# Strassen's seven block products in w2: two loaded summands move into the hi and lo pools, and the last product changes place

## The chip, the cores and the metric

The kernel runs on one core of a Trainium2 chip. The metric is the time of one execution on the device in microseconds (us), as the median of three runs. Five engines work beside each other: TensorE (PE in the profile) multiplies matrices, VectorE (DVE) and ScalarE (ACT) do element-wise work, GpSimd (POOL) does some copies and issues accumulating loads, and SyncE (SP) issues most of the transfers.

## The reference

The reference is a decoder trunk of two layers over 256 tokens of width 1024, all in float32. A layer is a gated feed-forward block (FFN), a mixer (a gated spatial unit beside differential attention), and a second FFN, each followed by a layer norm with a scaled residual:

```
def _swiglu(x, w1, w3, w2):
    return (jax.nn.silu(x @ w1) * (x @ w3)) @ w2
...
h = _swiglu(x, ffn_w1[l, 0], ffn_w3[l, 0], ffn_w2[l, 0])
x = _layernorm(ALPHA * x + 0.5 * h, ln_g[l, 0], ln_b[l, 0])
```

The hidden width is 2816, that is 22 blocks of 128. This document is about the last product of an FFN, `h @ w2`, with h of 256 x 2816 and w2 of 2816 x 1024. It is computed four times in an execution: in the FFN before and the FFN after the mixer of each of the two layers. They are called FFN 1 to FFN 4 here, in order of time.

## The kernel before

Every float32 weight is multiplied as a sum of two rounded parts. A piece of weights (128 x 1024 values) is loaded into a raw buffer; ACT copies it into a rounded high part, "hi" (L195 and L247 in the profile), and DVE subtracts that from the raw piece and leaves the rest, "lo" (L197 and L249). PE then makes three products: hi with the activations' high part, lo with the high part, hi with the low part. The hi and lo pieces live in two pools, `hi_pool` and `lo_pool`, of eight buffers each (HL = 8); a buffer is free again when the last matmul that reads it is done. The raw buffers are four.

`gemm_seven` (L377 on) computes `h @ w2`. The first eight of the 22 hidden blocks are treated as 2 x 2 blocks and are multiplied by Strassen's algorithm in seven block products (`product`, L369, matmuls on L373) in place of eight; the other 14 blocks are multiplied in the ordinary way (`rows`, L397, matmuls on L402). The output has two halves of 512 columns. In the first half of the stage, block products alternate with `between()`, which multiplies one of the seven ordinary pieces of the first output half (12 matmuls for both groups of 128 tokens, as many as a block product has). They are called P1 to P7 and b1 to b7 here, and the order on PE is

P1 b1 P2 b2 P3 b3 P4 b4 P5 b5 P6 b6 P7 b7, then `done` for the first output half, then the seven ordinary pieces of the second output half (`held`, 84 matmuls).

P1 uses the weights w11 and P2 w21. P3 needs w11+w12 and P4 w11+w12+w22, which DVE adds up in place (`plus`, L356) in the raw buffer r1. For that w12 is loaded as r2 and w22 as r3 (L419 and L426). P5 uses r3 itself, P6 uses r2 after w22 has been added to it by an accumulating transfer that POOL issues (`gather`, L350), and P7 uses r1 after w21 has been added to it in the same manner (L433). So r1, r2 and r3 are loaded tiles that live long.

Before the change r2 and r3 have buffers outside the pools, made in `ffn` under the name `spare`: r2 has two tiles with the tag "val" in the pool `act`, which earlier in the FFN hold results whose halves are transposed; r3 has one tile with the tag "x" in the pool `xs`, which holds half of the FFN's input until the last matmul that reads it. `spare` appears as a tile in the profile. In the first product of an FFN (`seven`, L837) the tiles that correspond to r2 and r3 already live in `hi_pool` and `lo_pool`.

Before a w2 stage stands `gemm_a2` for the two last blocks of w1 and w3: four pieces, whose hi parts are all multiplied first (L295, 32 matmuls) and whose lo parts come after that (L302, 32 matmuls). Before these are the last ordinary pieces of the first product (L283).

The partial sums P1, P3, P4, P6 and P7 are added to the residual in `Norm.fold` (L605, `xtok<-xtok,sbank`, on DVE). P1, P4, P6 and P7 go into the same PSUM bank `bx`, one after the other: what P6 leaves there, `fold` reads, and P7 is then accumulated into the same bank. The matmuls of P7 cannot start before the fold behind P6 has read the bank.

What sets the order of the work: PE runs its instructions in the order in which they are written. On the other engines a planner places the instructions by priorities (`step()` counts them up with each load) and by its own model of when data and buffers are there; a load issues when the planner has a buffer for it, and then waits on the chip until the last reader of that buffer is done. Within the products of an FFN the planner is bound by hand: `line` (L148) chains every hi piece on ACT behind the hi piece before it, and every lo piece and every `plus` on DVE behind the one before it, in the order written. So a `plus` that waits for its load holds up all later lo pieces. The folds, the work on h and the norm are not in this chain; the planner puts them where it expects room. SP issues loads and transposing transfers (L220) from one queue in the planner's order.

`setup` (L539) is a small task of the first FFN alone: it issues loads of constants, then yields, and after 16 beats it computes some constants (L552 to L566). A beat is a count of written matmul work: one block product or one `between()` is one beat.

Of the kernel before, what the change touches and what calls it, by code (L numbers as in the profile page):

```python
# [11 lines left out]
F32 = mybir.dt.float32  # L12
# [8 lines left out]
P = 128  # L21
D = 1024
# [15 lines left out]
HC = CH // 2  # L38
# [16 lines left out]
def trunk(ctx, tc, x, xT, w13a, w13b, w2, wb, wqk, wu, wg, wgr, wbr, wbrr, wo, gateb, gatebr, sgug, sgub, sguwT, sgubias, lam, diffg,  # L55
# [7 lines left out]
    hi_pool = ctx.enter_context(tc.tile_pool(name="hi", bufs=HL))  # L63
    lo_pool = ctx.enter_context(tc.tile_pool(name="lo", bufs=HL))
    xs = ctx.enter_context(tc.tile_pool(name="xs", bufs=2))
# [8 lines left out]
    def name(s):  # L74
        serial[0] += 1
        return f"{s}_{serial[0]}"
# [82 lines left out]
    def fetch(src, width=CH, raw=None):  # L159

        step()
        if raw is None:
            raw = raw_pool.tile([P, CH], F32, tag="raw", name=name("raw"))
        for g in gate:
            g[0] -= 1
        while len(gate) > 1 and gate[1][0] < 0:
            gate.pop(0)
        with behind(gate[0][1] if gate and gate[0][0] < 0 else None):
            if isinstance(raw, list):
                for j, v in enumerate(raw):  # L170
                    loaded[0] = nc.sync.dma_start(v, src[:, j * HC : (j + 1) * HC]).ins
            else:
                loaded[0] = nc.sync.dma_start(raw[:, :width], src).ins
        return raw
# [149 lines left out]
    def gemm_b(src, kts, xh, xl, done, tail=4, last=()):  # L324
# [13 lines left out]
        for t in range(NT):  # L338
            for ps, o, n in blocks[t]:
                for k, piece in held:  # L340
                    rows_b(ps, t, k, piece, xh, xl, kts, o, n)
                done(t, ps[:, :n], o, n)

    def halved(v):
        return v if isinstance(v, list) else [v[:, o : o + HC] for o in range(0, CH, HC)]

# [12 lines left out]
    def pieces(raw):  # L359
        out = []  # L360
        for v in halved(raw):
            hi = hi_pool.tile([P, HC], F32R, tag="hi", name=name("whi"))
            lo = lo_pool.tile([P, HC], F32R, tag="lo", name=name("wlo"))
            for eng, ins in zip((A, V), split(hi, lo, v, after=line[:2])):
                inline(eng, ins)
            out.append((hi, lo))
        return out

    def product(ps, x, w, start, stop):  # L369
        for k in range(4):  # L370
            hi, lo = (v[:, k % 2 * 512 : k % 2 * 512 + 512] for v in w[k // 2])
            for n, (y, o) in enumerate(((hi, 0), (lo, 0), (hi, 1))):
                PE.matmul(ps, x[o](k), y, start=start and k == n == 0, stop=stop and k == 3 and n == 2,  # L373
                          skip_group_check=True)
            beat(0.25)

    def gemm_seven(src, xh, xl, sums, spare, ln, done):  # L377

        q = [[bank(), bank()], [side_bank(), bank()]]
        bx, bz = side_bank(), q[1][0]
        (w11, w21), (w12, w22) = ([s[:, o : o + CH] for o in (0, CH)] for s in src)

        def rest(c):
            for k in range(8, FT, 4):
                nk = min(4, FT - k)
                for j, piece in enumerate(stream(src[c][:, k * 512 : (k + nk) * 512], nk * 512)):
                    yield k + 2 * j, piece

        def rows(t, c, k0, piece, o=0, n=512):  # L397
            for j in range(2):
                k = k0 + j
                hi, lo = (w[:, j * 512 + o : j * 512 + o + n] for w in piece)  # L400
                for m, (y, x) in enumerate(((hi, xh), (lo, xh), (hi, xl))):
                    PE.matmul(q[c][t][:, :n] if o == 0 else more[:, :n], x(k, t), y,  # L402
                              start=k == 8 and m == 0 and (c, t) != (1, 0), stop=k == FT - 1 and m == 2, skip_group_check=True)
            beat(n / 1024)

        def block(t, k0):
            return tuple(lambda k, f=f: f(k0 + k, t) for f in (xh, xl))

        a11, a12, a22 = block(0, 0), block(0, 4), block(1, 4)
        first = rest(0)  # L410

        def between():
            k, piece = next(first)
            for t in range(NT):
                rows(t, 0, k, piece)

        r1 = fetch(w11)
        p1 = pieces(r1)
        r2 = fetch(w12, raw=spare[0])  # L419
        plus(r1, r2)  # L420
        product(bx, a11, p1, True, False)
        ln.fold(0, 0, bx, ALU.add, True)
        between()
        product(q[0][0], a12, pieces(fetch(w21)), False, False)
        gather(r2, w22)
        r3 = fetch(w22, raw=spare[1])  # L426
        between()
        product(bz, sums[0], pieces(r1), True, False)
        ln.fold(1, 1, bz, ALU.add, True)
        between()  # L430
        product(bx, sums[1], pieces(plus(r1, r3)), False, False)
        ln.fold(0, 1, bx, ALU.subtract, True)
        gather(r1, w21)  # L433
        between()
        product(bz, sums[3], pieces(r3), False, False)
        between()
        product(bx, sums[2], pieces(r2), False, False)
        ln.fold(1, 1, bx, ALU.subtract, False)
        between()
        product(bx, a22, pieces(r1), False, True)  # L440
        ln.fold(1, 0, bx, ALU.add, True)
        between()
        for t in range(NT):
            done(t, q[0][t], 0, 512)
        held = list(rest(1))
        line[:] = None, None, False
        cuts = ((0, 512),), (((0, 256), (256, 256)) if ln.last else ((0, 512),))
        for t in range(NT):
            for o, n in cuts[t]:
                more = bank() if o else None  # L450
                for k, piece in held:
                    rows(t, 1, k, piece, o, n)
                done(t, (more if o else q[1][t])[:, :n], 512 + o, n)
# [85 lines left out]
    def setup(after):  # L539
        G.memset(mask[:, :P], 0.0)  # L540
        make_causal_mask(nc, mask[:, P:], NEG)
        lam_t = s512("lam").rearrange("p (l f d) -> p l f d", l=DEPTH, f=4)
        for dst, src in ((x_tok[0], x[:P, :]), (x_tok[1], x[P:, :]), (cos_t, cosT), (sin_t, sinT), (dgs, diffg),
                         (gbh, gateb), (ln_g, lngT), (ln_b, lnbT), (lam_t, lam.partition_broadcast(P))):
            first = dst
            while len(first.shape) > 2:
                first = first[:, 0]
            V.tensor_copy(first[:, :1], after)
            G.dma_start(dst, src)
        yield 16  # L550
        with behind(added[0]):
            V.tensor_scalar(out=gbh, in0=gbh, scalar1=0.5, scalar2=None, op0=ALU.mult)  # L552
        pr = s512("lampr").rearrange("p (l f d) -> p l f d", l=DEPTH, f=4)[:, :, :2]
        for j in range(2):
            with behind(added[0]):
                V.tensor_tensor(out=pr[:, :, j], in0=lam_t[:, :, 2 * j], in1=lam_t[:, :, 2 * j + 1], op=ALU.mult)
        ls = const.tile([P, DEPTH, 2], F32, name="ls")
        V.tensor_reduce(out=ls, in_=pr, op=ALU.add, axis=AX.X)
        A.activation(ls, ls, AF.Exp)
        for l in range(DEPTH):  # L560
            nl = const.tile([P, 1], F32, name=f"neg_lam{l}")
            V.tensor_scalar(out=nl, in0=ls[:, l, 1:2], scalar1=ls[:, l, 0:1], scalar2=-lambda_init(l),
                            op0=ALU.subtract, op1=ALU.add)
            neg_lam.append(nl)
            with behind(added[0]):
                V.tensor_scalar(out=dgs[:, l : l + 1], in0=dgs[:, l : l + 1], scalar1=1.0 - lambda_init(l),  # L566
                                scalar2=None, op0=ALU.mult)
# [175 lines left out]
    def ffn(l, f, i, norm, last=False):  # L743
        xh, xl = parts(both)
# [92 lines left out]
        def seven(src, x_sums):  # L837
# [18 lines left out]
            yield  # L856
            if norm:
                crossed(fetch(w21))
            r2 = fetch(w12, raw=[hi_pool.tile([P, HC], F32, tag="hi", name=name("r2")) for _ in range(2)])
            if norm:  # L860
                yield
            product(bz, x_sums[0], pieces(plus(r1, r2)), True, False)
            A.activation(v1, bz, AF.Copy)
            r3 = fetch(w22, raw=[lo_pool.tile([P, HC], F32, tag="lo", name=name("r3")) for _ in range(2)])
            yield
            product(bx, x_sums[1], pieces(plus(r1, r3)), False, False)
            A.activation(v0, bx, AF.Copy)
# [50 lines left out]
        for j in range(FA, FT - 4, 2):  # L918
            for m, z in gemm_a2([w13a[l, f, j - FA + m] for m in range(2)], both, lambda m: t512("silu")):
# [1 line left out]
                silu[0] = A.activation(s, s, AF.Silu).ins  # L921
                V.tensor_tensor(out=s, in0=s, in1=z[:, T:], op=ALU.mult)
                split(*(v[-1][:, (j - FA + m) * T : (j - FA + m + 1) * T] for v in (h_hi, h_lo)), s)
        spare = [[act.tile([P, D], F32, tag="val", name=name("spare"), bufs=2) for _ in range(2)],
                 xs.tile([P, 4, 512], F32, tag="x", name=name("spare")).rearrange("p k c -> p (k c)")]
        ln = Norm(l, i, 2.0 * ALPHA, 4.0 * EPS, s[:, :1], last)

        def done(t, p, c, n):
# [1 line left out]
            if c + n == D:  # L930
                ln.finish(t, 1.9)

        gemm_seven([w2[l, f, c] for c in range(2)], hh, hl, sums, spare, ln, done)
        return ln.close()

    def mixer(l, i, norm):
# [388 lines left out]
```

## Time and profile before

| | us |
|---|---|
| median of three runs | 1199.31 |
| lowest and highest run | 1195.99, 1201.52 |
| the profiled execution, its own time | 1200.3 |
| its span | 1198.5 |
| PE busy, of the span | 1183.9 |
| DVE busy, of the span | 1012.1 |
| ACT busy, of the span | 824.7 |

The profiled execution lies within the range of the runs, 1.0 us above their median. Some 1.8 us of its time lie outside the span. PE is busy for 99% of the span with a granted clock of 0.999, so time can be found only where PE waits, or in work that PE need not do. A busy time of 512-column matmuls counts overlapping matmuls once; the chain of waits has 12 of them, one block product, in 2.72 us, so in steady work one starts 0.227 us after the other.

The views used below: the waits of an engine (who waited for whom, with total, number and longest); the timeline (start, length, engine, line, and in brackets the idle time just before it and what ended it); the chain of work that ended last (start, length, what); and the table of stretches (busy time of each engine between two times).

### The profile page before, as it was taken

Reading aid. Unit: us, or ns where it says so; the run is one execution under the profiler, and the core shown is the slowest. Engines: PE = TensorE matmul, PEld = TensorE weight load, DVE = VectorE, ACT = ScalarE, POOL = GpSimd, SP = SyncE. Lnnn points to the kernel's source line nnn. Section 1 sums busy time; section 2 is a strip of 40 time slices with the busy share of each in tenths; the row PEclk is TensorE's granted clock in tenths of the full one; section 3 lists DMA queues with packets and bytes.
Section 4 is the critical chain, followed back from the end, with each engine's and each line's share of the span. In section 5 each row is a group of like instructions: output and inputs, shape, how many; then the busy total and the mean of one; then the engine's idle time right before and its main releaser. Section 6 shows DMA issues by size and latency. Waiting matters only on the chain.

```text
span 1198.5 us, 16639 instructions
## 1 busy us (share of the span) xinstructions
PE 1183.9 (99%) x5771; PEld 993.0 (83%) x5771; DVE 1012.1 (84%) x1558; ACT 824.7 (69%) x1418; POOL 299.4 (25%) x356
## 2 busy tenths in 40 slices
PE   9999999999999999999999999999999999999998
PEld 7888778888888888887788888888888888888877
DVE  6889989888688989879899879888965989989795
ACT  6688658559955677885677886576788556679860
POOL 1112301137430220071020071003564112102500
PEclk9999999999999999999999999999999999999999
DMA  9969885757855758698668698676666754886870
GB/s 350 284 193 283 257 285 192 265 198 212 248 205 186 226 180 272 198 284 241 240 205 270 173 290 253 230 270 239 210 204 211 252 182 165 259 252 212 269 236 36
DMA packets 129220, 276.14 MB, mean 230 GB/s; under 512 B 89024, under 2 KB 90096, under 8 KB 104560
## 3 DMA queue, kind: packets, MB, share of 16 engines
q1 hardware_dynamic: 121392, 248.80, 62.3%
q0 software_dynamic: 7312, 25.76, 9.1%
q8 instruction: 45, 0.74, 0.2%
q10 hardware_dynamic: 432, 0.52, 0.1%
q14 instruction: 39, 0.32, 0.1%
HBM read 249.10 MB, written 1.05 MB: 209 GB/s over the span
## 4 chain that ended last, share of the span: by engine, by line
PE 84%; DMA 6%; DVE 5%; ACT 3%; issue 1%; POOL 0%; SPq 0%; ACTq 0%; DVEq 0%; POOLq 0%
PE bank L283 43%; PE bank L295 13%; PE sbank L373 8%; PE bank L302 7%; PE bank L402 6%; PE sbank L402 3%; DMA raw<-in_w 3%; DVE wlo L197 2%; PE bank L512 2%; PE sbank L984 1%; DMA spare<-in_w 1%; DVE wlo L249 1%; DMA planes<-planes 1%; ACT whi L195 1%; ACT whi L247 1%
## 5 line engine op out<-in xcount | busy, mean ns | idle before, releaser
L197 DVE TENSOR_TENSOR wlo<-raw,whi 128x1024 fp32r<-128x1024 f32 (+1 forms) x374 | 414.5, 1136 | 52.5 <-ACT whi L195 38.1
L195 ACT ACTIVATE whi<-raw 128x1024 fp32r<-128x1024 f32 (+1 forms) x378 | 351.8, 959 | 135.1 <-PE bank L283 43.7
L283 PE MATMUL bank<-whi,x 128*128 128x512 f32 x1224 | 386.3, 390 | 0.0
L283 PEld LDWEIGHTS bank<-whi,x 128*128 128x128 f32 x1224 | 229.8, 188 | 47.8
L283 PE MATMUL bank<-wlo,x 128*128 128x512 f32 x612 | 238.2, 389 | 0.0
L295 PE MATMUL bank<-x,whi 128*128 128x512 f32 x640 | 153.3, 391 | 0.0
L295 PEld LDWEIGHTS bank<-x,whi 128*128 128x128 f32 x640 | 118.2, 188 | 23.8
L283 PEld LDWEIGHTS bank<-wlo,x 128*128 128x128 f32 x612 | 114.9, 188 | 23.2
L247 ACT ACTIVATE whi<-raw 128x1024 fp32r<-128x1024 f32 (+1 forms) x96 | 92.4, 983 | 60.2 <-DVE raw L356 35.1
L249 DVE TENSOR_TENSOR wlo<-raw,whi 128x1024 fp32r<-128x1024 f32 (+1 forms) x96 | 110.1, 1161 | 12.5 <-ACT whi L247 12.3
L229 POOL COPY seven<-seven 128x512 uint16<-128x512 uint16 x16 | 67.1, 4253 | 105.9 <-ACT whi L195 54.5
L302 PEld LDWEIGHTS bank<-x,wlo 128*128 128x128 f32 x640 | 81.4, 191 | 2.9
L302 PE MATMUL bank<-x,wlo 128*128 128x256 f32 x640 | 82.6, 283 | 0.0
L402 PE MATMUL bank<-whi,hhi 128*128 128x512 f32 (+1 forms) x182 | 68.3, 375 | 0.8 <-DVE silu L305 0.8
L402 PE MATMUL bank<-whi,hlo 128*128 128x512 f32 (+1 forms) x182 | 67.9, 373 | 0.0
L402 PE MATMUL bank<-wlo,hhi 128*128 128x512 f32 (+1 forms) x182 | 67.9, 373 | 0.0
L960 POOL TENSOR_TENSOR swap<-swap,sin_t 128x512 f32<-128x512 f32 x16 | 25.9, 1618 | 103.4 <-DMA swap<-z 59.3
L719 POOL COPY nvia<-ntwo 128x256 uint16<-128x256 uint16 x20 | 9.9, 539 | 159.1 <-DMA ntwo<-nvia 108.0
L303 ACT ACTIVATE r<-bank 128x256 f32<-128x256 f32 x96 | 34.0, 372 | 12.9 <-PE bank L302 12.8
L373 PE MATMUL sbank<-whi,xhs 128*128 128x512 f32 x128 | 42.0, 389 | 0.0
L402 PEld LDWEIGHTS bank<-whi,hhi 128*128 128x128 f32 x182 | 34.3, 188 | 7.2 <-DVE silu L305 1.3
L402 PEld LDWEIGHTS bank<-whi,hlo 128*128 128x128 f32 x182 | 34.3, 188 | 6.1
(286 smaller groups left out, 2159.1 us busy)
## 6 DMA issues: line engine op xcount, KB each, us to landing
raw<-in_w13b SPq DMA_DIRECT2D x68, 1024.0 KB, 5.5
raw<-in_w SPq DMA_DIRECT2D x32, 1024.0 KB, 6.4
raw<-in_wb SPq DMA_DIRECT2D x16, 1024.0 KB, 5.5
raw<-in_wqk SPq DMA_DIRECT2D x16, 1024.0 KB, 5.7
r<-in_w13b SPq DMA_DIRECT2D x16, 512.0 KB, 5.9
raw<-in_w13a SPq DMA_DIRECT2D x8, 1024.0 KB, 4.8
raw<-in_wgr SPq DMA_DIRECT2D x8, 1024.0 KB, 5.4
raw<-in_wg SPq DMA_DIRECT2D x8, 1024.0 KB, 5.1
```

What stands on the lines that cost most here:

```text
L195: inline(A, A.activation(h, r, AF.Copy).ins)
L197: low = eng.tensor_tensor(out=w, in0=r, in1=h.bitcast(F32), op=ALU.subtract).ins
L229: eng.tensor_copy(out=o, in_=i)
L247: a = A.activation(hi, src, AF.Copy).ins
L249: return a, eng.tensor_tensor(out=lo, in0=src, in1=hi.bitcast(F32), op=ALU.subtract).ins
L283: PE.matmul(ps, xx, w, start=start and n == 0, stop=stop and n == 2)
L295: PE.matmul(b[-1], hi[:, k * P : (k + 1) * P], xc(k), start=k == 0, stop=False)
L302: PE.matmul(b[n][:, :T], lo[:, k * P : (k + 1) * P], xc(k)[:, :T], start=False, stop=k == KT - 1)
L303: emptied[0] = A.activation(r[:, s], b[n][:, T:], AF.Copy, scale=scale).ins
L373: PE.matmul(ps, x[o](k), y, start=start and k == n == 0, stop=stop and k == 3 and n == 2, skip_group_check=True)
L402: PE.matmul(q[c][t][:, :n] if o == 0 else more[:, :n], x(k, t), y, start=k == 8 and m == 0 and (c, t) != (1, 0), stop=k == FT - 1 and m == ...
L960: turned_by[0] = G.tensor_tensor(out=s3, in0=s3, in1=s, op=ALU.mult).ins
```

## The change

It has three parts. First, the tiles of r2 (two of 128 x 1024) are taken from `hi_pool` and those of r3 (two of 128 x 1024) from `lo_pool`, by a new function `homes`; `spare` and its three tiles go. r3 is then loaded by two transfers of 512 KB in place of one of 1 MB. `seven` calls the same function for the tiles that it already had there, which changes nothing in it. Second, `between()` with b7 stands ahead of P7, so that the order on PE becomes ... P6 b6 b7 P7, `done`, `held`. Third, `setup` yields for 22 beats in place of 16.

```diff
+    def homes(pool, tag):
+        return [pool.tile([P, HC], F32, tag=tag, name=name("home")) for _ in range(2)]
...
-    def gemm_seven(src, xh, xl, sums, spare, ln, done):
+    def gemm_seven(src, xh, xl, sums, ln, done):
...
         p1 = pieces(r1)
-        r2 = fetch(w12, raw=spare[0])
+        r2 = fetch(w12, raw=homes(hi_pool, "hi"))
         plus(r1, r2)
...
         gather(r2, w22)
-        r3 = fetch(w22, raw=spare[1])
+        r3 = fetch(w22, raw=homes(lo_pool, "lo"))
         between()
...
         product(bx, sums[2], pieces(r2), False, False)
         ln.fold(1, 1, bx, ALU.subtract, False)
         between()
+        between()
         product(bx, a22, pieces(r1), False, True)
         ln.fold(1, 0, bx, ALU.add, True)
-        between()
         for t in range(NT):
             done(t, q[0][t], 0, 512)
...
-        yield 16
+        yield 22
         with behind(added[0]):
             V.tensor_scalar(out=gbh, in0=gbh, scalar1=0.5, scalar2=None, op0=ALU.mult)
...
-        spare = [[act.tile([P, D], F32, tag="val", name=name("spare"), bufs=2) for _ in range(2)],
-                 xs.tile([P, 4, 512], F32, tag="x", name=name("spare")).rearrange("p k c -> p (k c)")]
...
-        gemm_seven([w2[l, f, c] for c in range(2)], hh, hl, sums, spare, ln, done)
+        gemm_seven([w2[l, f, c] for c in range(2)], hh, hl, sums, ln, done)
```

More of the change, by code (lines that the diff above doesn't have):

```diff
@@ L858, in seven @@
                 crossed(fetch(w21))
-            r2 = fetch(w12, raw=[hi_pool.tile([P, HC], F32, tag="hi", name=name("r2")) for _ in range(2)])
+            r2 = fetch(w12, raw=homes(hi_pool, "hi"))
             if norm:
@@ L863, in seven @@
             A.activation(v1, bz, AF.Copy)
-            r3 = fetch(w22, raw=[lo_pool.tile([P, HC], F32, tag="lo", name=name("r3")) for _ in range(2)])
+            r3 = fetch(w22, raw=homes(lo_pool, "lo"))
             yield
```

## The prediction

> **What bounds the kernel now.** I read the busy times first, then who PE waited for, then a table of the four w2 stages, and then the chain and the timeline in them. The page's row of busy times says that PE is busy nearly all the time:
>
> ```profile
> PE 1183.9 (99%) x5771; PEld 993.0 (83%) x5771; DVE 1012.1 (84%) x1558; ACT 824.7 (69%) x1418; POOL 299.4 (25%) x356
> ```
>
> The change removes no matmul, so it can only win back PE's waits. Whom PE waited for (total, number, longest):
>
> ```profile
> PE sbank L373 <- DVE xtok L605: 3.4, 3, 1.4
> ...
> PE sbank L373 <- ACT whi L247: 1.3, 1, 1.3
> PE sbank L373 <- DVE wlo L249: 1.2, 2, 0.8
> ...
> PE bank L402 <- DVE silu L305: 0.8, 1, 0.8
> ```
>
> All four rows lie in `product` and `rows`, that is in w2 stages (L373 is shared with the FFN's first product). How much each stage loses comes from four stretches, each from the first matmul of P1 to the first matmul behind the stage (FFN 1 to FFN 4; length, then PE, PEld, DVE, ACT, POOL):
>
> ```profile
> 124.50:186.69 62.19, 58.76 (x258) 47.47 (x257) 54.59 (x84) 38.45 (x58) 7.67 (x9) 1.00 0.75 254
> 540.57:602.39 61.82, 59.03 (x259) 47.55 (x258) 55.52 (x78) 36.23 (x54) 5.08 (x7) 1.00 0.72 234
> 719.60:777.51 57.91, 57.91 (x259) 47.79 (x258) 52.94 (x76) 34.85 (x52) 3.01 (x6) 1.00 0.76 250
> 1131.12:1190.34 59.22, 58.42 (x297) 49.27 (x296) 47.70 (x68) 25.88 (x35) 3.40 (x6) 1.00 0.51 160
> ```
>
> FFN 3 has no idle PE at all: 57.91 us is the stage's floor at the same granted clock of 1.00. Against it FFN 1 loses 4.28, FFN 2 3.91 and FFN 4 1.31 us (its last tile is cut in two, so a little of that is not a wait). Together 9.5 us: that is the ceiling of any gain here, 0.8% of the kernel.
>
> **Part one: b7 ahead of P7.** The chain of waits shows what holds P7 up in FFN 2 (start, length, what):
>
> ```profile
> 560.93 8.54 DMA raw<-in_w
> ...
> 569.55 1.07 ACT whi L247
> ...
> 571.79 1.74 DVE wlo L197 x2
> ...
> 574.06 2.35 DVE wlo L197 x2
> 576.42 0.61 DVE xtok L605
> ...
> 577.16 2.97 PE sbank L373 x12
> 580.13 2.72 PE bank L402 x12
> ```
>
> The accumulating load into r1 lands 8.54 us after its issue; P7's pieces, which are ahead of b7's in the chained order, wait for it, the following pieces pile up behind, and the fold behind P6 runs only after four of them. P7 needs the bank that this fold reads. Its own pieces, done before the 571.79 us row, had been ready for five microseconds. The same wait in FFN 1 and FFN 4, as the timeline gives it:
>
> ```profile
> 161.63 0.47 PE L373 MATMUL sbank<-whi,hhi 128*128 128x512 f32 x1 [1.34 <-DVE xtok L605]
> ...
> 577.16 0.47 PE L373 MATMUL sbank<-whi,hhi 128*128 128x512 f32 x1 [1.41 <-DVE xtok L605]
> ...
> 1165.22 0.47 PE L373 MATMUL sbank<-whi,hhi 128*128 128x512 f32 x1 [0.61 <-DVE xtok L605]
> ```
>
> Idle 3.36 us in all. With b7 in between, P7 is due 2.72 us later (the 12 matmuls of b7 in the chain above), so a fold that keeps its place is done 1.3 us ahead of need in FFN 2 (2.72 less the wait of 1.41). Term one: -3.4 us. Bounds: -3.4, and 0 if the planner moves the fold back by as much.
>
> What moves with it: b7's load, its hi and lo now precede P7's two pieces in the chain, which takes DVE's idle time in front of the late load away, and b7 no longer waits for it. The cover is ample: in the chain above b7's lo starts at 571.79, and b7 is now due at 575.6 (576.96 less the wait of 1.41 us). r1's raw buffer is given up some 2 us later, so one load for the second output half goes out that much later on SP; its piece is due only after several others of 12 matmuls each. On POOL nothing is passed. `fold`, then both `part`s, come in one burst on DVE behind P7, five operations with their statistics at 0.61 us (the fold's row) or little more, while PE runs 84 matmuls on other banks: hidden; without that cover some 3 us. I take 0.
>
> **Part two: r2 and r3 in the pools.** In FFN 2 the second tile of r2 becomes free late, and DVE stands still until its load has come:
>
> ```profile
> 531.55 1.23 DVE L356 TENSOR_TENSOR raw<-raw,spare 128x1024 f32<-128x1024 f32 x1 [0.57 <-DMA spare<-in_w]
> ...
> 534.36 0.57 SPq L171 DMA_DIRECT2D spare<-in_w  x1
> ...
> 540.44 1.23 DVE L356 TENSOR_TENSOR raw<-raw,spare 128x1024 f32<-128x1024 f32 x1 [7.07 <-DMA spare<-in_w]
> ...
> 717.10 1.23 DVE L356 TENSOR_TENSOR raw<-raw,spare 128x1024 f32<-128x1024 f32 x1 [5.26 <-DMA spare<-in_w]
> ```
>
> The last row is FFN 3. There the load comes 2.50 us ahead of P1's start (717.10 against 719.60), in FFN 2 0.13 us ahead (540.44 against 540.57): 2.37 us later, and FFN 2's loss beside the fold is 3.91 - 1.41 = 2.50 us. So DVE's lateness goes into PE's time one for one.
>
> With the change r2 needs two of eight hi buffers. Ahead of it in written order stand four pieces of `gemm_a2` and two of P1; the other two are those of the matmuls on L283, which end where L295 begins. From the chain (FFN 3):
>
> ```profile
> 708.68 7.25 PE bank L295 x32
> 715.93 3.83 PE bank L302 x32
> ```
>
> So the second load of r2 can leave SP by 708.7 in FFN 3, and by the same distance, 10.9 us ahead of P1 (719.60 - 708.68), at 529.6 in FFN 2 in place of 534.36: 4.7 us sooner. That is more than the 2.37 us which FFN 2 lacks. I take -2.0 there, -0.5 in FFN 4 (1.31 less 0.61, not all a wait), 0 in FFN 3. Bounds: -2.5 and -0.7; on the other side a later r2, priced as a rival below.
>
> r3 now needs two lo buffers, free when the pieces of L302 are read, in place of the input's tile, which is free after all of L302. Its two loads are each half as long:
>
> ```profile
> spare<-in_w SPq DMA_DIRECT2D x8, 512.0 KB, 5.9
> ...
> spare<-in_w SPq DMA_DIRECT2D x4, 1024.0 KB, 9.4
> ```
>
> They land some 3.5 us sooner (9.4 - 5.9). PE waits for r3 nowhere, so 0; one issue more on SP is some 0.57 us (the issue's row above) of SP's queue, in which no load stands that PE waits for here.
>
> The cost: six hi buffers for the pieces while r2 lives, and six lo buffers while r3 does. P4's second piece then takes the hi buffer that b2 gives up. b2 ends one product and one `between()` ahead, so the buffer is free 5.4 us (2 x 2.72) before P4 starts; ACT's 1.07 and some 1.2 of DVE (1.74 and 2.35 us for two, in the chain) make 2.3 us. Every later piece has at least as much. So 0, with 2.3 us for each pair of pieces as the price if that cover goes.
>
> The trace has one more price. A lo piece takes 1.21 us, but in FFN 1 the one that starts at 119.5, while POOL copies until 120.2, takes 1.73:
>
> ```profile
> L197 DVE TENSOR_TENSOR wlo<-raw,whi x2: 1212/1470/1727, 119.5 to 121.2; 128x1024 fp32r<-128x1024 f32 x2
> ...
> 117.67 2.57 POOL L229 COPY seven<-seven 128x512 uint16<-128x512 uint16 x2 [3.37 <-DMA seven<-seven]
> ...
> 712.57 2.85 POOL L229 COPY planes<-planes 128x512 uint16<-128x512 uint16 x4
> ```
>
> In FFN 3 POOL's four copies (the last row) fall into the 5.26 us in which DVE stands still, in FFN 2 and 4 likewise; the sooner load puts DVE's work there. Four operations longer by 0.52 us make 2.1 us of DVE, inside the time gained. I take 0.5 us for PE in FFN 2 to 4 together (0 to 2.1 each).
>
> [...]
>
> **Part three: `setup` six beats later.** Today its operations stand in DVE's queue ahead of P4's sum, in FFN 1, and P4 waits for that:
>
> ```profile
> 129.53 0.41 DVE L552 TENSOR_SCALAR gbh<-gbh 128x32 f32<-128x32 f32 x1
> 129.80 0.20 DVE L566 TENSOR_SCALAR dgs<-dgs 128x1 f32<-128x1 f32 x2
> ...
> 133.03 0.48 DVE L556 TENSOR_TENSOR lampr<-lam 128x128 f32<-128x128 f32 x2
> ...
> 133.77 0.41 DVE L558 TENSOR_REDUCE ls<-lampr 128x4 f32<-128x256 f32 x1
> ...
> 137.75 0.33 DVE L562 TENSOR_SCALAR neg_lam<-ls 128x1 f32<-128x1 f32 x2
> ...
> 142.26 0.50 PE L373 MATMUL sbank<-whi,sum 128*128 128x512 f32 x1 [1.25 <-ACT whi L247]
> 143.53 0.50 PE L373 MATMUL sbank<-wlo,sum 128*128 128x512 f32 x1 [0.76 <-DVE wlo L249]
> ```
>
> 0.41 + 0.20 + 0.48 + 0.41 + 0.33 = 1.83 us of DVE. Six beats are three block products and three `between()`s, 16 us, so they come at about 146 us, behind P4's pieces. FFN 1's loss beside the fold is 4.28 - 1.34 = 2.94 us. Against this, r2 comes later here: its second load leaves by 111.14 us today, and with hi buffers by 113.6, 10.9 us ahead of P1's 124.50. The rows are the issue (with its length to the end of the second), the two sums, and DVE's idle time before P4:
>
> ```profile
> 107.34 3.80 SPq L171 DMA_DIRECT2D spare<-in_w  x2
> ...
> 116.74 2.88 DVE L356 TENSOR_TENSOR raw<-raw,spare 128x1024 f32<-128x1024 f32 x2
> ...
> 132.69 0.42 DVE L249 TENSOR_TENSOR hlo<-silu,hhi 128x256 fp32r<-128x256 f32 x1 [1.22 <-ACT hhi L247]
> ```
>
> The delay of 2.5 us meets 1.22 us in which DVE stands still, so 1.3 us remain. I take -1.8 + 1.3 = -0.5 us, and -0.9 more for the short gaps within P4 (2.94 less 1.25 and 0.76), which a P4 with pieces at hand does not have: -1.4. Bounds -2.9 and +1.3.
>
> **Sum.** -3.4 - 2.0 - 0.5 + 0.5 - 1.4 = -6.8 us. I allow +0.6 for restarts of a planner's order that I cannot see, one wait like the smallest above (0.61): -6.2. The profiled execution took 1200.3, so 1194.1 on its own time; it lies 1.0 above the median of 1199.31, so the median to expect is 1193.1.
>
> **The rivals.** (A) *r2 comes later, not sooner.* The planner may hand r2 the last hi buffers, those that L295 reads, and not those of L283. Its second load then leaves when L295 ends: in FFN 2 at 536.9, 3.7 us ahead of P1 (719.60 - 715.93), against 534.36 today: 2.5 us later. In FFN 3 it leaves at 715.93; today, with the 6.1 us that the load takes in FFN 2 (534.36 to 540.44), at 711.0: 4.9 later, and the same in FFN 4. In FFN 1 at 120.8 against 111.14: 9.7. Together 22.0 us, passed on one for one, less 3.4 and 1.8: 1200.3 + 16.8 = 1217. For it: a load competes with conversions that the planner would rather have early. Against: r2's load has no data to wait for, and the FFN's first product keeps such tiles in these pools with no wait of PE in the table above. It ends slower by 0.5% if r2 is later by 3 us on average over the four stages (12 us, less 5.2 of gains, is over 6.0). (B) *Only the fold's wait is won.* DVE is busy 55.52 of 61.82 us in FFN 2; if it stays the limit, P4's waits come back at b3 or P5: 1200.3 - 3.4 = 1196.9, a median of 1196. Against: FFN 3 has DVE work of 52.94 and no wait. (C) *The move does nothing.* The fold is not chained, and the planner may put it as far back as P7 went: only parts two and three remain, -3.4 + 0.6, so 1197.5 and a median of 1196.5.
>
> **How the numbers follow.** Forecast 0.60, A 0.15, B 0.16, C 0.09. A measurement of this kernel tells about 0.5%, 6.0 us, from no change. The forecast's own width is 1189.8 (the ceiling of 9.5 us) to 1196, and 0.37 of its 0.60 lie below 1193.3; its other 0.23, B, C and 0.03 of A, where r2 is late by a little, are within 0.5%; 0.12 of A is slower. That makes 0.37, 0.51, 0.12. The range runs from the ceiling, 1189.8, to 1202, which takes in B and C and the mild end of A and leaves out some 0.15.
>
> **What would show it.** P7's first matmul without a wait for L605; DVE's waits for r2's load, 7.07 and 5.26 us in FFN 2 and 3, below 2; r2's second load leaving SP no later than L295's start; P4 in FFN 1 waiting under 1.5 us; the four stretches at 58 to 60 us. The forecast is wrong if a stretch other than FFN 1 exceeds 60 us, if ACT's or DVE's pieces wait for matmuls of L295 or b2 while PE waits for them, or if FFN 3, which has nothing to win, becomes longer by over 1 us.

## The result and the profile after

| | before | after |
|---|---|---|
| median, us (20 runs each) | 1201.52 | 1195.28 |
| lowest and highest run | 1195.99, 1207.13 | 1193.83, 1197.62 |
| ratio of after to before | | 0.995, interval 0.9936 to 0.9963 |
| the profiled execution, its own time | 1200.3 | 1197.46 |
| its span | 1198.5 | 1195.7 |

The change won 6.2 us, 0.5%, and the runs lie closer together: 3.8 us apart instead of 11.1. The before kernel's median was 1199.31 over its first three runs and is 1201.52 over twenty. The profiled execution of after is one of its slowest, 2.2 us above its median: its losses are not those of every execution.

On the page of after the row of busy times shows as many matmuls as before, and PE busy for 1.4 us longer:

```profile
PE 1185.3 (99%) x5771; PEld 994.5 (83%) x5771; DVE 1012.0 (85%) x1558; ACT 826.2 (69%) x1418; POOL 286.1 (24%) x356
```

Of the waits of PE these two are all that is left in the w2 stages (total, number, longest). No row names the fold any more (it was L605 and is L608 now):

```profile
PE bank L376 <- DVE wlo L249: 3.9, 3, 1.9
...
PE sbank L376 <- DVE wlo L249: 0.6, 1, 0.6
```

The table of the same four stretches, each from P1 to the end of the stage (length, then PE, PEld, DVE, ACT, POOL, the granted clock, the share of DMA, GB/s):

```profile
124.14:185.50 61.36, 58.78 (x259) 47.38 (x257) 56.35 (x87) 38.48 (x56) 4.76 (x7) 1.00 0.77 245
539.51:597.22 57.71, 57.71 (x258) 47.63 (x257) 52.98 (x76) 36.20 (x53) 4.47 (x7) 1.00 0.79 251
714.55:772.50 57.95, 57.95 (x259) 47.63 (x258) 53.21 (x77) 35.86 (x51) 3.28 (x5) 1.00 0.78 251
1126.27:1188.14 61.87, 59.91 (x297) 50.47 (x296) 50.21 (x70) 28.18 (x35) 4.20 (x6) 0.97 0.52 158
```

FFN 2 fell from 61.82 to 57.71 and now has no idle PE. FFN 3 stayed. FFN 1 fell by only 0.83, and FFN 4 *rose*, from 59.22 to 61.87. Together the stages won 2.3 of the span's 2.8 us. Where a stage is said to lose so much below, it is the sum over its matmuls of what each starts later than at the steady spacing (0.227 us for 512 columns, 0.12 for 256); by that, to about 0.1 us, FFN 1 to 4 lost 4.6, 3.9, 0.1 and 1.5 us before and 3.7, 0.1, 0.3 and 4.1 after.

What FFN 4 lost is a new wait at P2, and something behind it. The timeline of PE (start, length, what, and the idle time before with what ended it) and the table of 4 us stretches around it:

```profile
1133.46 0.40 PE L376 MATMUL bank<-whi,hhi 128*128 128x512 f32 x1
1135.74 0.50 PE L376 MATMUL bank<-wlo,hhi 128*128 128x512 f32 x1 [1.89 <-DVE wlo L249]
...
1137.11 0.63 PE L376 MATMUL bank<-whi,hlo 128*128 128x512 f32 x1
1137.54 0.63 PE L405 MATMUL bank<-whi,hhi 128*128 128x512 f32 x1
```

```profile
1132.00:1136.00 4.00, 2.04 (x8) 1.31 (x8) 3.88 (x9) 3.99 (x8) 0.00 (x0) 1.00 0.97 350
1136.00:1140.00 4.00, 4.00 (x12) 3.09 (x12) 4.00 (x6) 1.80 (x2) 1.10 (x2) 0.57 1.03 395
```

P2's second piece has no lo part yet, and PE stands still for 1.89 us. Then the matmuls start 0.43 us apart instead of 0.23: the granted clock over the second stretch of 4 us is 0.57. Some eight matmuls, each 0.2 us late, make the extra 1.6 us, and they count as busy time.

Why the lo part is late is seen on SP's queue, here in FFN 2 and in FFN 4:

```profile
527.26 0.33 SPq L171 DMA_DIRECT2D home<-in_w  x1
528.37 4.00 SPq L220 DMA_TRANSPOSE planes<-planes  x2
532.49 0.50 SPq L171 DMA_DIRECT2D home<-in_w  x1
```

```profile
1114.02 0.33 SPq L171 DMA_DIRECT2D home<-in_w  x1
1115.64 4.71 SPq L220 DMA_TRANSPOSE planes<-planes  x2
1120.45 0.53 SPq L171 DMA_DIRECT2D home<-in_w  x1
```

and on VectorE at the sum that waits for the second load:

```profile
536.17 2.19 DVE L359 TENSOR_TENSOR raw<-raw,home 128x1024 f32<-128x1024 f32 x1 [2.38 <-DMA home<-in_w]
```

```profile
1125.76 1.23 DVE L359 TENSOR_TENSOR raw<-raw,home 128x1024 f32<-128x1024 f32 x1 [3.90 <-DMA home<-in_w]
```

The second load of r2 stands behind two transposing transfers on SP, and goes out 0.1 us after the second of these has been issued. In FFN 2 that is 7.02 us ahead of P1, in FFN 4 5.82. The sum then starts 3.34 us ahead of P1 in FFN 2 and 0.51 us ahead in FFN 4 (1126.27 - 1125.76). Every lo piece behind it in the chained order is late with it. In FFN 1 P2 waits in the same way (idle 0.95 and 1.01 us); there the second load went out 6.5 us ahead of P1:

```profile
117.59 0.53 SPq L171 DMA_DIRECT2D home<-in_w  x1
...
130.95 0.50 PE L376 MATMUL bank<-wlo,hhi 128*128 128x512 f32 x1 [0.95 <-DVE wlo L249]
...
133.62 0.49 PE L376 MATMUL bank<-wlo,hhi 128*128 128x512 f32 x1 [1.01 <-DVE wlo L249]
```

### The profile page after: what moved, and what is told of

Read it like the earlier page. It is cut to its first block, busy times and chain, and to the rows that moved or that the text cites. A ratio compares the mean times of both kernels' runs of the same rounds, so it can differ in the third digit from the quotient of the medians.

```text
span 1195.7 us, 16657 instructions
## 1 busy us (share of the span) xinstructions
PE 1185.3 (99%) x5771; PEld 994.5 (83%) x5771; DVE 1012.0 (85%) x1558; ACT 826.2 (69%) x1418; POOL 286.1 (24%) x356
## 4 chain that ended last, share of the span: by engine, by line
PE 92%; DVE 4%; DMA 2%; issue 1%; ACT 1%; SPq 0%; DVEq 0%; ACTq 0%
PE bank L283 44%; PE bank L295 14%; PE sbank L376 10%; PE bank L405 9%; PE bank L302 7%; PE sbank L405 3%; PE bank L515 1%; DVE wlo L197 1%; PE sbank L985 1%; DMA home<-in_w 1%; DVE wlo L249 1%; DMA raw<-in_w13b 1%; PE bank L376 1%; PE sbank L1041 1%; PE sbank L1159 1%
## 5 line engine op out<-in xcount | busy, mean ns | idle before, releaser
L197 DVE TENSOR_TENSOR wlo<-raw,whi 128x1024 fp32r<-128x1024 f32 (+1 forms) x374 | 414.7, 1134 | 52.8 <-ACT whi L195 38.0
L283 PE MATMUL bank<-whi,x 128*128 128x512 f32 x1224 | 386.5, 390 | 0.0
L283 PEld LDWEIGHTS bank<-whi,x 128*128 128x128 f32 x1224 | 229.8, 188 | 47.7
L283 PE MATMUL bank<-wlo,x 128*128 128x512 f32 x612 | 238.3, 389 | 0.0
L295 PE MATMUL bank<-x,whi 128*128 128x512 f32 x640 | 153.3, 391 | 0.0
L295 PEld LDWEIGHTS bank<-x,whi 128*128 128x128 f32 x640 | 118.2, 188 | 23.8
L283 PEld LDWEIGHTS bank<-wlo,x 128*128 128x128 f32 x612 | 114.9, 188 | 23.4
L229 POOL COPY seven<-seven 128x512 uint16<-128x512 uint16 x16 | 55.9, 3554 | 115.6 <-ACT whi L195 60.8
L359 DVE TENSOR_TENSOR raw<-raw,home 128x1024 f32<-128x1024 f32 x32 | 40.4, 1273 | 25.1 <-DMA home<-in_w 22.0
```

The costliest lines, as they stand in the source:

```text
L197: low = eng.tensor_tensor(out=w, in0=r, in1=h.bitcast(F32), op=ALU.subtract).ins
L229: eng.tensor_copy(out=o, in_=i)
L283: PE.matmul(ps, xx, w, start=start and n == 0, stop=stop and n == 2)
L295: PE.matmul(b[-1], hi[:, k * P : (k + 1) * P], xc(k), start=k == 0, stop=False)
L359: inline(V, V.tensor_tensor(out=v, in0=v, in1=m, op=ALU.add).ins)
```

## The experiments

Each kernel was run in five rounds. Ratios are to the before kernel on the same chip, with their 95% interval.

**Each part alone.** First the move of b7, on the before kernel:

```diff
+        between()
         product(bx, a22, pieces(r1), False, True)
         ln.fold(1, 0, bx, ALU.add, True)
-        between()
```

> The kernel before with b7 ahead of P7 and nothing else changed. Theory (the parts add up): P7's waits for the fold (idle 1.34, 1.41 and 0.61 us in FFN 1, 2 and 4 before) are gone and all other waits stay: 3.4 to 3.8 us less, ratio 0.997. Rival (the planner moves the fold back by one piece as well): P7 still waits for L605 by more than 1 us in two stages, no change.

Measured: 1197.53 us, 0.9964 (0.994 to 0.9987), that is -4.3 us, with runs from 1191.75 to 1202.32. No stage has a wait at P7. The profiled execution, 1200.51 us, is above its median: in FFN 3 r2's load came late (its sum waited for it until 717.13, P1 had begun at 715.83), and b1 waited. The bank that b1 writes is read first by L305, which stands on VectorE behind that sum and two lo pieces:

```profile
721.02 0.50 PE L402 MATMUL bank<-whi,hhi 128*128 128x512 f32 x1 [2.28 <-DVE silu L305]
```

Then `setup` alone on the before kernel:

```diff
-        yield 16
+        yield 22
```

> The kernel before with setup's pause of 22 beats in place of 16 and nothing else changed. Theory (its 1.8 us of VectorE stand ahead of P4's sum): P4 in FFN 1 waits 2.0 us less or so and the other stages are as before: 1 to 2 us less, ratio 0.999. Rival (VectorE is late at P4 for other reasons): P4's two waits of 1.25 and 0.76 us stay, no change.

Measured: 1201.41 us, 1.0006 (0.9984 to 1.0027). No change that can be told. In FFN 1 what P4 lost did fall, from 2.7 to 1.0 us, but r2's load was late in FFN 3 and FFN 4 of this execution, and b1 waited there for 1.1 and 2.7 us.

Then the homes of r2 and r3 alone (`homes` and its calls from the change's diff, with b7 and the 16 beats as before):

```diff
-        r2 = fetch(w12, raw=spare[0])
+        r2 = fetch(w12, raw=homes(hi_pool, "hi"))
...
-        r3 = fetch(w22, raw=spare[1])
+        r3 = fetch(w22, raw=homes(lo_pool, "lo"))
```

> The kernel before with r2 and r3 in the pools and nothing else changed. As predicted (r2 never later than today but in FFN 1, by 2.5 us): 2 to 3 us less, FFN 2's stretch shorter by 2 us and more, FFN 4 not longer. Theory from the trace after (the planner puts r2's second load behind the transposing transfers on SP's queue, so r2 comes 5 to 6 us later against P1 in FFN 1 and 2 us later in FFN 4): P2 waits 2 us or so in FFN 1 and again in FFN 4, FFN 2 gains 2 to 2.5 us, so 0 to 3 us more, ratio 1.000 to 1.002.

Measured: 1199.92 us, 0.9987 (0.9969 to 1.0006), runs from 1197.29 to 1201.47. In the waits of PE the fold is still there, and the waits at P2 have come:

```profile
PE bank L376 <- DVE wlo L249: 3.3, 2, 2.3
PE sbank L376 <- DVE xtok L608: 2.7, 3, 1.3
```

So the three parts alone are worth -4.3, +0.7 and -1.6 us by their ratios (0.9964, 1.0006 and 0.9987 of 1201.5). They add up to -5.2, within the interval of the whole change (-7.7 to -4.4). The move is the one part whose gain alone can be told from nothing.

**One part undone.** The move undone in the after kernel (b7 behind P7 again):

> The changed kernel with b7 back behind P7. Theory: P7 waits for the fold again in two to four stages, 3 to 4.5 us more than the changed kernel's 1195.3, 1198.5 to 1200. Rival (with r2 earlier VectorE is ahead anyway and the fold is in time): 1195.3.

Measured: 1198.83 us, 0.9979 (0.9963 to 0.9994), 3.5 us above the after kernel. The fold's waits are back:

```profile
PE sbank L376 <- DVE xtok L608: 1.9, 2, 1.3
```

`setup` undone (`yield 22` to `yield 16` in the after kernel):

> The changed kernel with setup's pause of 16 beats as before. Theory (its 1.8 us of VectorE come back ahead of P2 to P4 in FFN 1, as the kernel with the pools alone has them): FFN 1 loses 5 to 6 us in place of 3.7, and with a wait of more than 2 us the halved clock for 3.4 us, 1196.5 to 1198. Rival (no part of it matters): 1195.3.

Measured: 1195.58 us, 0.9957 (0.994 to 0.9974). My number of 1196.5 and more was wrong: the six beats bring nothing that can be told here. The timeline of VectorE in FFN 1 of the after kernel suggests why:

```profile
138.74 0.17 DVE L555 TENSOR_SCALAR gbh<-gbh 128x32 f32<-128x32 f32 x1
...
139.69 1.22 DVE L359 TENSOR_TENSOR raw<-raw,home 128x1024 f32<-128x1024 f32 x1
...
141.42 0.33 DVE L565 TENSOR_SCALAR neg_lam<-ls 128x1 f32<-128x1 f32 x2
141.66 1.22 DVE L359 TENSOR_TENSOR raw<-raw,home 128x1024 f32<-128x1024 f32 x1
```

The planner did not put `setup` behind P4's sums (139.69 and 141.66) but right ahead of the first and between the two. It still stands in P4's way; it only stands there closer.

r2 back in the two "val" tiles, the rest as in the after kernel:

```diff
-        r2 = fetch(w12, raw=homes(hi_pool, "hi"))
+        r2 = fetch(w12, raw=spare)
...
+        spare = [act.tile([P, D], F32, tag="val", name=name("spare"), bufs=2) for _ in range(2)]
```

> The changed kernel with r2 back in the two tiles of the pool act, r3 still in lo_pool. Theory (what the pools bring is r2's steadier and mostly earlier landing): r2's second sum falls anywhere from 2.6 us before P1's start to 2 us after it, b1 or P4 wait again by 1 to 3 us in one or two stages, median 1197 to 1198 and single runs more than 6 us apart. Rival (r3's earlier load is what counts): as the changed kernel, 1195.3.

Measured: 1200.1 us, 0.9996 (0.9974 to 1.0018), with runs from 1195.13 to 1207.5. So r2's home is worth 4.8 us beside the other parts, more than I gave it. The profiled execution shows where it goes: FFN 1 is better than in the after kernel (0.8 us lost against 3.7), FFN 4 has

```profile
1128.31 1.23 DVE L359 TENSOR_TENSOR raw<-raw,spare 128x1024 f32<-128x1024 f32 x1 [8.36 <-DMA spare<-in_w]
```

with P1 at 1127.11, and PE waits at b1 for 2.2 us; the granted clock over 1126 to 1188 us is 0.97, in the other stages 1.00. This kernel has the move too, and yet is no faster than before, where the move alone won 4.3 us. The two intervals overlap between 0.9974 and 0.9987; whether r3's home or `setup` costs something while r2 is in the "val" tiles was not run. One thing that differs from a good stage is how long the transposing transfers ahead of the load take. The table of DMA issues in a short stretch has the median time from issue to landing in its last column; here it is for FFN 4 of this kernel:

```profile
spare<-in_w SPq DMA_DIRECT2D x1, 512.0 KB, 7.4
planes<-planes SPq DMA_TRANSPOSE x2, 6.1
```

for FFN 2 of the before kernel, where VectorE stood still for 7.07 us:

```profile
spare<-in_w SPq DMA_DIRECT2D x1, 512.0 KB, 6.0
planes<-planes SPq DMA_TRANSPOSE x2, 6.3
```

and for its FFN 3, where the sum was in time:

```profile
spare<-in_w SPq DMA_DIRECT2D x2, 512.0 KB, 5.5
...
planes<-planes SPq DMA_TRANSPOSE x2, 3.4
```

The transposing transfers take 3.4 us or 6.3 in one and the same execution, and r2's load goes out behind them. The load itself takes longer too: the second of the two in FFN 3 landed in 5.1 us (the 5.5 is the median of both), that of FFN 2 in 6.0. Over all kernels the spread of the runs goes with r2's home: with r2 in the "val" tiles it is 11.1, 10.6, 10.0 and 12.4 us (before, the move alone, `setup` alone, this one), with r2 in the hi pool 1.1 to 6.3 us (all the others), over 6 to 20 runs each. That r2's late load is behind the spread in the runs without a profile is an inference.

r3 back in the tile of `xs` (one load of 1 MB), the rest as in the after kernel:

```diff
-        r3 = fetch(w22, raw=homes(lo_pool, "lo"))
+        r3 = fetch(w22, raw=spare)
```

> The changed kernel with r3 back in the tile of the pool xs, loaded in one piece of 1 MB, r2 in hi_pool. Theory (PE waits for r3 nowhere): as the changed kernel, 1195.3 within 1 us. Rival (with r2 earlier, VectorE reaches P4's sum before r3 has landed): P4 waits by 1 us or more in FFN 2 or 3, over 1196.5.

Measured: 1197.49 us, 0.9963 (0.9949 to 0.9977); the intervals of this and of the after kernel overlap. I had expected no difference beyond 1 us, and it came out 2.2 us slower. The profiled execution's waits are at P2 and P4 in FFN 1 and in FFN 4. The loss is thus not only where r3 is used, and its cause stays open.

**r2's load ahead of the transposing transfers.** If the queue on SP is what makes r2 late, then a load that is written ahead of P1's pieces, and so is planned before the transposing transfers, should take P2's waits away:

```diff
         r1 = fetch(w11)
-        p1 = pieces(r1)
         r2 = fetch(w12, raw=homes(hi_pool, "hi"))
+        p1 = pieces(r1)
```

> The changed kernel with r2 fetched ahead of P1's conversions, so that r2 takes the earlier hi buffers and both its loads stand ahead of the transposing transfers on SP's queue. Theory (r2's late landing is what P2 waits for in FFN 1 and FFN 4): the sum of w11+w12 starts 4 to 6 us earlier against P1, the waits at P2 are gone, 3 to 5 us less than the changed kernel's 1195.3, ratio 0.991 to 0.993 to the kernel before. Rival (VectorE's own work ahead of P2 is the cause): P2 waits as before, 1195. Second rival (P1's pieces, now behind r2, come late): P1 waits instead, over 1195.

Measured: 1193.59 us, 0.9943 (0.992 to 0.9966), with runs only 1.1 us apart. Both loads now leave together, 16.3 us ahead of P1 in all four stages; in FFN 2:

```profile
523.48 1.30 SPq L171 DMA_DIRECT2D home<-in_w  x2
...
529.07 1.23 SPq L220 DMA_TRANSPOSE planes<-planes  x1
```

P2 waits in no stage, and FFN 2 to 4 lose no more than 0.1 us each. FFN 1 lost 4.7, in a new way: b1 waits for L305 to have read its bank, and on VectorE L305 stands behind a lo piece that ran while GpSimd copied (the second row is a summary of line L197: shortest, median and longest, in ns):

```profile
130.10 0.50 PE L405 MATMUL bank<-whi,hhi 128*128 128x512 f32 x1 [2.71 <-DVE silu L305]
```

```profile
L197 DVE TENSOR_TENSOR wlo<-raw,whi x2: 1214/2696/4179, 123.3 to 124.4; 128x1024 fp32r<-128x1024 f32 x2
```

```profile
124.44 3.10 POOL L229 COPY planes<-planes 128x512 uint16<-128x512 uint16 x4
```

The subtraction that starts at 124.4 takes 4.18 us instead of 1.21, and ends 1.0 us behind the last of the four copies.

**The copies moved from GpSimd to ACT**, on top of the last kernel (L792 of the after kernel: who joins the halves of the last front):

```diff
-  yield from transposed(s, p, s, lead, wait - lead, 2.6, A if n < 3 else G, to, A if n else G)
+  yield from transposed(s, p, s, lead, wait - lead, 2.6, A if n != 3 else G, to, A if n else G)
```

> The kernel that fetches r2 first, with the last front's four copies after its transposing transfers on ScalarE in place of GpSimd. Theory (a VectorE subtraction waits out GpSimd's copies: 4.18 us in place of 1.21 ahead of b1 in FFN 1): b1's wait of 2.9 us in FFN 1 and the halved clock behind it are gone, no VectorE subtraction above 2 us there, 3 to 4.5 us less than the 1193.6 of that kernel, 1189 to 1190.5. Rival (VectorE is late at b1 for its own work, or ScalarE now is): FFN 1 keeps a wait of 2 us or more, 1193 and over.

Measured: 1192.46 us, 0.9931 (0.9914 to 0.9948). The wait at b1 is gone, and the two subtractions take what they take elsewhere:

```profile
122.69 2.35 DVE L197 TENSOR_TENSOR wlo<-raw,whi 128x1024 fp32r<-128x1024 f32 x2
```

The four stretches of this execution, in the same columns as above, are all but at the floor except for FFN 1, where P4 still waits for 1.3 us:

```profile
124.62:183.85 59.23, 58.29 (x259) 47.54 (x257) 54.14 (x85) 40.83 (x62) 4.24 (x6) 1.00 0.82 267
538.06:595.71 57.65, 57.65 (x259) 47.70 (x257) 50.60 (x74) 37.10 (x55) 4.26 (x6) 1.00 0.76 250
713.07:770.71 57.64, 57.64 (x258) 47.70 (x257) 50.57 (x73) 36.56 (x53) 2.83 (x4) 1.00 0.76 252
1124.49:1182.41 57.92, 57.92 (x296) 49.41 (x295) 46.11 (x66) 29.18 (x39) 3.37 (x5) 1.00 0.53 165
```

The median gained only 1.1 us on the kernel before it, less than I had expected. The same edit on the after kernel itself, with r2's load where it was:

> The changed kernel with the last front's four copies on ScalarE in place of GpSimd, r2 not fetched first. Theory (P2 waits in FFN 1 and FFN 4 because r2's second load stands behind the transposing transfers on SP's queue): r2's second load leaves 5.5 to 7 us ahead of P1 as in the changed kernel, P2 waits in FFN 1 by 1 us and more, 1194 to 1195.5. Rival (GpSimd's copies hold up VectorE there too): P2's waits are gone, 1192 to 1193.

Measured: 1193.51 us, 0.9936 (0.9914 to 0.9958), 1.8 us below the after kernel and a little better than I had given it. P2 in FFN 1 still starts late (by 0.7 and 1.2 us), as expected, but FFN 2 to 4 lose only 0.5, 0.1 and 0.8 us. VectorE's sums at r2's second load take 1.22 and 1.23 us there, where the after kernel's took 2.19 and 1.98 in FFN 2 and 3. By the medians both edits so bring 1 to 2 us each, in either order; the intervals overlap.

**All of it, and `setup` later still** (`yield 30` on top of the kernel with both edits):

> The kernel that fetches r2 first and has the copies on ScalarE, with setup's pause of 30 beats. Theory (its 1.8 us of VectorE are what is left ahead of P4 in FFN 1): P4's wait of 1.1 us is gone, 1 us less than that kernel's 1192.5. Rival (P4 waits for VectorE's other work): the wait stays, 1192.5.

Measured: 1191.29 us, 0.9915 (0.9891 to 0.9938), the fastest of all; its slowest run, 1193.66, is below the fastest of the after kernel, 1193.83. The profiled execution is that slowest one. In it P4 in FFN 1 waits for something else, r3's second load, and the clock halves again behind the wait (0.57 granted over 144 to 148 us):

```profile
140.94 1.22 DVE L359 TENSOR_TENSOR raw<-raw,home 128x1024 f32<-128x1024 f32 x1 [1.06 <-DMA home<-in_w]
```

```profile
143.55 0.50 PE L376 MATMUL sbank<-wlo,sum 128*128 128x512 f32 x1 [1.97 <-DVE wlo L249]
```

`setup` now lies mostly behind the two sums. The gain of 1.2 us over the kernel with 22 beats is within what the two intervals leave open.

## Why the prediction was right or wrong

The size of the gain came out as forecast, 6.2 us for 6.2. The median measured, 1195.28, is 2.2 us above the 1193.1 that I named, because the median of before that I counted from was itself 2.2 us low. The ratio is 0.995, and its interval leaves 1 out. That the total agrees to the tenth is luck, though. Part three's -1.4 came to nothing, P2's waits in FFN 1 and 4 and the clock are not in the sum, and against these r2's home is worth 4.8 us beside the other parts where part two had -2.0, for a reason that the prediction does not have.

*Part one was right.* P7's wait for the fold went in all stages. -3.4 us was the term; the move alone measured -4.3, and undoing it +3.5. The rival that the fold moves back with P7 is refuted by both. One figure in the working is in no row: P7's wait ends at 577.16, not 576.96, so b7 was due at 575.75; nothing hangs on the difference.

*Part two was right in FFN 2 and wrong in the step that led there.* FFN 2 lost 0.1 us in place of 3.9, of which the fold's wait was 1.4. But "the second load of r2 can leave SP ... 10.9 us ahead of P1" did not hold in any stage: it left 5.8 to 7.0 us ahead. I had asked when the buffer is free, and not what stands ahead of the load in SP's queue. Two transposing transfers do; the later of them carries the last front's product, which VectorE (L775) can take up only when L283 has ended, at 528.63 in FFN 2. The timeline of SP that I quoted for the before kernel shows the same load 0.06 us behind the same two transfers (529.43 plus 4.87 us is 534.30, and it left at 534.36), and I had left that row out. When the load was put ahead of them, it left 16.3 us ahead of P1, and P2's waits went. VectorE's waits for r2's load in FFN 2 and 3, 7.07 and 5.26 us before, fell to 2.38 and 2.73, not below 2 as I had written.

*Rival A's effect came in a mild form, by another way.* Not the buffers that L295 reads held r2's load back, but the transfers ahead of it in the queue. In FFN 1 r2's second load left 6.5 us ahead of P1 (124.14 - 117.59) where it had been 13.4 or more (124.50 less 111.14, the end of the row of two loads); P2 lost 2.3 us there. In FFN 4 it left 5.8 us ahead where it had been 7.7, and P2's second piece started 2.06 us late. I had named the stretch of over 60 us in FFN 4 as a sign against the forecast, and it came. In this execution the two stages together lose 7.8 us, where it was 6.1, although part one took 1.95 us out of them. FFN 1's share is the rule, FFN 4's is not: in the five other kernels with r2 in the hi pool and its load behind the transposing transfers (the homes alone, and the after kernel with r3 back, `setup` or the move undone, or the copies on ACT) the second load leaves 5.1 to 6.5 us ahead of P1 in FFN 1, but in FFN 4 the sum starts 2.6 to 3.1 us ahead of P1, not 0.5, and P2's second piece starts at most 1.0 us late.

*Where the rest of the gain was.* r2's home does not make its load leave much sooner: 0.8 us in FFN 2 (6.2 to 7.0 us ahead of P1), and 0.8 and 1.9 us later in FFN 3 and 4. It makes the load land sooner and within a narrower range. In FFN 2 to 4 of the profiled executions r2's second load takes 5.0 to 7.6 us from issue to landing with the "val" tiles (12 stages of four kernels) and 3.6 to 5.2 us in the hi pool behind the transposing transfers (18 stages of six kernels). One more thing goes with r2's home: the accumulating load of 512 KB that POOL issues into r2's first tile. With the "val" tiles it goes out 0.1 to 1.4 us ahead of r2's second load in each of the 12 stages, in the hi pool 1.8 to 2.7 us behind it in each of the 18. In FFN 2 before (r2's second load left at 534.36) and after (532.49):

```profile
533.39 0.85 POOL L350 DMA_DIRECT2D spare<-in_w  x1 [3.94 <-ACT whi L195]
...
535.03 0.83 POOL L353 DMA_DIRECT2D home<-in_w  x1
```

That this load holds the other up would fit, but no run moves it alone, and the second transposing transfer, which goes out before it, is steadier in the hi pool as well (3.9, 4.0 and 5.2 us to land in FFN 2 to 4 of after, against 6.6, 2.8 and 2.8 before). So that r2's home brings the gain is shown, by undoing it; what in it does so is open. I read the before kernel's single profile, with one bad stage in four, as the rule for FFN 2; in other executions the bad stage is FFN 3 or FFN 4, as the kernels with the "val" tiles show. Much of the gain is that executions with such a stage no longer occur. The fastest run of the move alone, 1191.75, is faster than any of the after kernel, so in good executions the other two parts may cost a little.

*The price of GpSimd's copies was too small.* I took 0.5 us, from a row of 1.73 us in place of 1.21. The longest rows were 1.98 and 2.19 us in the after kernel (FFN 3 and 2) and 4.18 in the kernel with r2's load first. With the copies on ACT they are back at 1.2, and the median gains 1.8 us on the after kernel, though the intervals overlap. In each of the three longest rows the extra length is close to the time that copies on GpSimd are recorded beside it: in the after kernel 0.96 us (2.19 less 1.23) beside 1.15 in FFN 2 (the sum from 536.17, copies until 537.32) and 0.75 beside 0.94 in FFN 3 (from 711.65, until 712.59), in the kernel with r2's load first 2.97 (4.18 less 1.21) beside 3.10. So the price was near the whole time beside the copies, where I had 0.52 us for an operation. What holds VectorE up was not shown, and which of the two came first cannot be read from the longest row, since the subtraction is recorded from 124.40 and the first copy from 124.44.

*Part three's term, -1.4, was wrong in its first step,* "they come at about 146 us": they came at 138.7 to 141.7, ahead of and between the sums. Undone, it changed the median by 0.3 us.

*Not in the sum at all* was the clock: the wait of 1.89 us in FFN 4 cost another 1.6. The allowance of 0.6 did not cover it in this execution.

## What to carry to other kernels

A buffer that was free sooner let its load leave at most 0.8 us sooner here while two transposing transfers stood ahead of it in its queue: it left 5.8 to 7.0 us ahead of P1, and 16.3 us ahead when it was written in front of them. Read the queue's own timeline up to the load, and where a slow transfer stands there, write the load ahead of it. One profile of a kernel whose runs spread by 1% shows one draw: ask which wait varies from stage to stage within it, since a change that takes the variation away is worth more than that one profile shows. The wait of PE of 1.89 us here had half a clock behind it, 1.6 us more, while waits of 2.28 and 2.33 us in other kernels had not: look at the granted clock behind a wait before you price it.

## What the runs showed of the hardware

- After some waits of PE of about 2 us and more the granted clock fell to a half, after others it did not. It did so behind 1.89 us (after, FFN 4: 0.50 over the next 3.41 us), 1.97 us (the kernel with `setup` at 30 beats, FFN 1: 0.57 over 144 to 148 us) and 2.71 us (r2's load first, FFN 1: 0.69 over 132 to 136 us), but not behind 2.28 us (the move alone, FFN 3: the matmuls behind it start 0.23 us apart) or 2.33 us (`setup` undone, FFN 1: 1.00 from 124 to 140 us). With the wait of 2.2 us (r2 back, FFN 4) it was 0.97 over 1126 to 1188 us. So the length of the wait alone does not decide it; what does was not shown. In the trace of the after kernel the clock falls to a half at 1136.38, is back at 1139.79, and falls to a half again at 1194.41, behind the last matmul. Here are the 3.41 us ahead of the first fall and the 3.41 us behind it, in the columns of the table of stretches; PE stands idle for 1.89 us of the first and has half the clock in the second:

```profile
1132.97:1136.38 3.41, 1.52 (x7) 0.92 (x6) 3.29 (x7) 3.41 (x6) 0.06 (x1) 1.00 0.95 372
1136.38:1139.79 3.41, 3.41 (x10) 2.63 (x9) 3.41 (x5) 1.42 (x2) 1.04 (x2) 0.50 1.01 392
```

- Two transposing transfers of the same size took 3.4 us (before, FFN 3 and 4) to 7.7 us (the move alone, FFN 3) from issue to landing, as the median of the two. What makes them slow is open; no run here isolates it.
- One subtraction on VectorE took 2.97 us longer beside four copies on GpSimd (4.18 us in place of 1.21); with these copies on ACT two of them took 2.35 us, no longer than elsewhere.
